# Page order of the second half's low-rank queries, and shorter planned waits in the scan, in a fused attention, delta-rule and memory layer

## The chip, the cores and the metric
One NeuronCore of a Trainium2 chip runs the whole layer in one launch. The metric is the device time of one execution in microseconds: the median of several runs, and beside it one profiled execution with a trace of every engine. The engines are named as in the profile: PE (TensorE), DVE (VectorE), ACT (ScalarE), POOL (GpSimd), and SP, which only issues DMAs here.

## The reference
The layer takes 2048 tokens of width 1024. After an RMS norm, one projection `h @ w_in` (about 4300 columns) gives the inputs of three groups of heads and a gate:

- **MLA attention**, 4 heads: queries through a low-rank step of 384 (`rms_norm(c_q) @ w_q_b`), keys and values through one of 256 (`rms_norm(c_kv) @ w_kv_b`), rotary parts, causal softmax.
- **Gated delta rule**, 4 heads: causal convolution and SiLU of q, k, v, l2 norms, a triangular solve for each chunk of tokens, and a scan over the chunks that carries a 128x128 state.
- **Memory attention**, 4 heads over 256 memory tokens, which have a norm and a projection of their own.

The three outputs are put side by side, multiplied by `silu(gate)`, projected by `w_out` and added to x; a last RMS norm follows. All is float32; the large products are made of three products of rounded high and low parts (`mm3`).

## The kernel before
The tokens are done in two halves (`hf` 0 and 1) of two blocks of 512. In each half, PE works through 34 jobs of the input projection (tile `ip`, 128 output columns each, two units of weights). What a job feeds runs beside it as a generator: `token_scalars`, `delta_head` (one for each head), `low_rank` for queries (n = 3) and for keys and values (n = 2), `mem_proj` once. Then come attention (`attention`, from `start_attention` on: scores `sc`, transposes `pt`, values `av`) and the output projection (`op`).

The order of the instructions is written out by a planner while the program is built. It keeps one clock for each engine (`T`), adds an estimated cost for each instruction, and after every three matmuls of the main stream `pump()` steps the generators whose time has come. A generator that says `yield d` comes back when its last results are due, plus d ns; one that lacks a resource says `yield POLL` and asks again 800 ns later. The engines then execute their queues in the order written; a matmul whose operand is late holds up all matmuls behind it. `SPARE` (line 43) is the d of the steps of the delta rule: three in each chunk of the scan (lines 1043, 1047, 1055), eight chunks in each head and half, and a few before and after it (lines 873, 914, 1078).

Buffers are counted. The counter `page` has 10 (tiles of 128x1024), `bw` has 1 (small weights), `scan`, `A` (rows of a head), `lt` (the solve's matrix) have 1. Whoever asks first and finds enough gets them; nothing is kept for anybody.

- A delta-rule head takes 2 pages with its q job and gives one back at the end of its scan and one after gating; its v job takes 1 for the time of its convolution (lines 1812 to 1815). `pick` takes the first job in the list whose needs are met, else a later one.
- `low_rank` takes 2n pages at once (line 1121): 6 for queries, 4 for keys and values, and `bw` for its second part; it gives both back at its end.
- `mem_proj` takes 4 pages and `bw` together (line 1236). It is started by the 44th pick (`MEM_AT`).
- The list of the second half begins with the scalars, heads 0 to 3, queries, keys and values (`LONG[1]` is "0123qk"), then gates and memory queries.

A head's own chain is: rows and `kk` matmuls, `lsys` written and read back as `lt`, 62 dependent steps on POOL (`pr`, `X`), `tsys` written and read back, two rounds of `mid` and `inv`, then the scan (`pa`), whose turn comes when the head before it is done. The tiles `lt`, `LT` and all pages share one ring of 16 buffers (line 940 and line 409).

Attention needs, for the first four MLA jobs (tokens of the first half), keys and values alone; the fifth job in order is one of memory attention, and its loader waits for the low-rank queries of all blocks:

```
while done.get("rows", 0) < 8 or "mem" not in done or ("rank", 3, 3) not in done:   # mem_loader, 1362
yield from until(("rank", 3, 3), ("rank", 2, 3), "mem")                            # hand_over, 1653
while done.get(("gdn", 1), 0) < NH:                                                # until_gdn, 1665
```

`hand_over` passes the buffers of the projection stage to attention in three steps, the last of them (6 pages among it) after the last delta-rule head.

Of the kernel before, what the change touches and what calls it, by code (L numbers as in the profile page):

```python
# [25 lines left out]
NH = 4  # L26
# [13 lines left out]
TRIG_AT = 1  # L40
MEM_AT = 44
STRICT = False
SPARE = 700.0
LONG = "012k3q", "0123qk"
CONV = 4
CBIAS = 2000.0
# [21 lines left out]
def hybrid_layer(ctx, tc, a, out):  # L68
# [6 lines left out]
    def dma(out, in_):  # L75
        nc.sync.dma_start(out=raw(out), in_=raw(in_))
# [250 lines left out]
    POLL = 800.0  # L327
# [22 lines left out]
    done = {}  # L350

    def can(**need):
        return all(avail[k] >= n for k, n in need.items())

    def grab(**need):
        assert can(**need)
        for k, n in need.items():
            avail[k] -= n

    def take(**need):  # L360
        while not can(**need):
            yield POLL
        grab(**need)

    def give(**need):
        for k, n in need.items():
            avail[k] += n
# [37 lines left out]
    def t2(name, shape=(P, 512), dtype=F32):  # L405
        return sb.tile(list(shape), dtype, name=name, tag="x2", bufs=14)

    def page(name):
        return sb.tile([P, HALF], F32, name=name, tag="page", bufs=16)
# [4 lines left out]
    def psg(name):  # L414
        return psum(name, "g")
# [58 lines left out]
    def rstd_of(acc, n):  # L474

        parts = yield from channel_rms(acc, n)
        return (yield from row_of(parts))
# [10 lines left out]
    def sumsq(xs, width=512):  # L488
        acc = t2("acc", (P, width))
        A.activation(acc, xs[0], AF.Square)  # L490
        for x in xs[1:]:
            sq = t2("sq", (P, width))
            A.activation(sq, x, AF.Square)
            V.tensor_tensor(acc, acc, sq, op=ALU.add)
        return acc
# [346 lines left out]

    def delta_head(hf, h, q, k, res):

        yield from take(N=1)
        sums, norms = (sb.tile([P, 16], F32, name=n, tag=n, bufs=b) for n, b in (("sums", 1), ("norms", 4)))
        for i in range(4):
# [24 lines left out]
        V.tensor_tensor(kfac, cols[:, 2:4, hs], nk.unsqueeze(1).broadcast_to([P, 2, 8]), op=ALU.mult)  # L872
        yield SPARE
        ps = psg("rn")
# [13 lines left out]
        def rows(b):  # L888
            return [row("fr", rows_n[hf, h, i * HALF + b * 512:i * HALF + (b + 1) * 512]) for i in range(3)]
# [6 lines left out]
        for b in range(2):  # L896
# [15 lines left out]
            if b == 0:  # L912
                cur = rows(1)
                yield SPARE
            for c2 in range(2):
# [32 lines left out]
        for j in range(31):  # L948
            n = j // 4 + 1
# [67 lines left out]
        for c in range(NCK):  # L1017
            cl = h * 8 + c
            if c % 4 == 0:
# [13 lines left out]
                else:  # L1033
# [8 lines left out]
                                   op0=ALU.mult, op1=ALU.add)  # L1042
            yield SPARE
            vn = sb.tile([P, P], F32, name="vn", tag="vn", bufs=2)
            PE.matmul(pa[:, 128:256], TT[:, c, :], r, start=True, stop=True)
            A.copy(vn, pa[:, 128:256])
            yield SPARE
            PE.matmul(pa[:, 256:384], kt[:, c % 4, :], vn, start=True, stop=True)
# [5 lines left out]
            step_end[0] = t  # L1054
            yield SPARE
        give(scan=1, P2=1, TT=1, page=1)
# [14 lines left out]
        for b in range(2):  # L1071
# [5 lines left out]
            V.tensor_tensor(ob3, ob3, inv_ro[:, b * 4:b * 4 + 4].unsqueeze(2).broadcast_to([P, 4, P]), op=ALU.mult)  # L1077
            yield SPARE
            ps = psg("oT")
# [11 lines left out]
    def small_weights(srcs):  # L1091

        def load(src):
            w = sb.tile([P, src.shape[1]], F32, name="bw", tag="m2", bufs=9)
            dma(out=w, in_=src, awaited=False)
            return w

        def split(w):
            n = w.shape[1]
            wh = sb.tile([P, n], F32R, name="bwh", tag="m2", bufs=9)  # L1100
            copy(wh, w)
            wl = sb.tile([P, n], F32R, name="bwl", tag="m2", bufs=9)
            lesser("bwl").tensor_tensor(wl, w, wh, op=ALU.subtract)
            return wh, wl
        w = load(srcs[0])
        yield 2800
        cur = split(w)
        w = load(srcs[1])
        yield 0
        for i in range(len(srcs)):  # L1110
            nxt = None
            if i + 1 < len(srcs):
                nxt = split(w)
                if i + 2 < len(srcs):
                    w = load(srcs[i + 2])
            yield cur
            cur = nxt

    def low_rank(hf, n, gain, srcs, use):

        yield from take(page=2 * n)
        hs, ls = ([[], []] for _ in range(2))
        for b in range(2):
            yield from take(t2=n)
            raws = [t2("craw") for _ in range(n)]
            for i in range(n):
                dma(out=raws[i], in_=craw_d[n][i][hf * 2 + b])
            yield 0
            acc = sumsq(raws)
            yield 0  # L1130
            r = yield from rstd_of(acc, n * P)
            for i in range(n):
                c = raws[i]
                V.scalar_tensor_tensor(c, c, gain[:, i:i + 1], r, op0=ALU.mult, op1=ALU.mult)
                hl = page("chl").bitcast(F32R)
                hi, lo = hl[:, 0:512], hl[:, 512:1024]
                A.copy(hi, c)
                V.tensor_tensor(lo, c, hi, op=ALU.subtract)
                hs[b].append(hi)
                ls[b].append(lo)  # L1140
                yield 0
            give(t2=n)
        yield from take(bw=1)
        t = 0
        for w in small_weights(srcs):
            if isinstance(w, tuple):
                yield from use(hf, t, hs, ls, *w)
                t += 1
                yield 0
            else:  # L1150
                yield w
        give(bw=1)
        for b in range(2):
            done[("rank", n, hf * 2 + b)] = True
        give(page=2 * n)
# [654 lines left out]
    def head_jobs(hf, h, res):  # L1810
        q, k, v = [], [], []
        return [Job(T_GDN + h, conv_consume(hf, h, q), dict(page=2, x2=2)),
                Job(T_GDN + 4 + h, conv_consume(hf, 4 + h, k), dict(x2=2),
                    after=lambda: spawn(delta_head(hf, h, q[0], k[0], res))),
                Job(T_GDN + 8 + h, conv_consume(hf, 8 + h, v), dict(x2=2, page=1))]

    def rank_jobs(hf, t0, n, gain, srcs, use):
        js = []
        for i in range(n):
            def consume(b, ps, i=i):  # L1820
                t = t2("craw")
                whole(hf, b, t, ps)
                dma(out=craw_d[n][i][hf * 2 + b], in_=t)
            js.append(Job(t0 + i, consume))
        js[-1].after = lambda: spawn(low_rank(hf, n, gain, srcs, use))
        return js
# [370 lines left out]
```

## Time and profile before

| | |
|---|---|
| three runs, us | 1817.6, 1817.95, 1824.83 (median 1817.95) |
| profiled execution, us | 1822.34 |
| its span, us | 1820.6 |
| mean granted TensorE clock | 0.983 |
| busy, share of span | PE 96%, PE weight load 81%, DVE 64%, ACT 40%, POOL 27% |
| instructions | 28632 |

Busy time of PE is the union of pipelined matmuls; where a stretch of 50 us shows less than 50 us, PE stood idle. The granted clock has two levels, 1.00 (2.4 GHz) and 0.50 (1.2 GHz); a figure between them is a mean over a stretch.

### The profile page before, as it was taken

What the parts mean: (1) busy time and instruction counts of PE and PEld (TensorE: products, weight loads), DVE (VectorE), ACT (ScalarE), POOL (GpSimd) and SP (SyncE); (2) the same over time, 40 slices, a digit from 0 to 9 for tenths busy, and PEclk for the clock granted to TensorE, in tenths of its full rate; (3) what the DMA queues carried; (4) which work ended last, traced back from release to release, by engine and by line L of the source; (5) the groups of instructions that cost most, each with busy time, mean ns of one, the idle gap of its engine ahead of it and who ended that gap; (6) DMA issues with size and microseconds to landing.
All of it is one profiled execution on the core that took longest, in us unless ns stands there. A gap on an engine that the chain in (4) does not pass through costs nothing.

```text
span 1820.6 us, 28632 instructions
## 1 busy us (share of the span) xinstructions
PE 1746.9 (96%) x9776; PEld 1471.2 (81%) x9776; DVE 1158.6 (64%) x2622; ACT 734.6 (40%) x1884; POOL 500.4 (27%) x894
## 2 busy tenths in 40 slices
PE   7999999999999999899999997999999999999998
PEld 5778788888777777788888876899999998888886
DVE  6777766786785858445566653777676778345443
ACT  6444233342442535213453423455455556222121
POOL 1422752443521124352112625001111012412120
PEclk9999999999999999999999998999999999999999
DMA  7544474456555344564555479145252527566551
GB/s 265 163 128 150 137 237 137 131 160 211 154 170 176 121 147 116 184 194 138 182 199 176 141 216 265 61 127 178 70 177 71 159 88 224 167 195 199 168 162 53
DMA packets 225826, 291.19 MB, mean 160 GB/s; under 512 B 30320, under 2 KB 130672, under 8 KB 225680
## 3 DMA queue, kind: packets, MB, share of 16 engines
q1 hardware_dynamic: 218640, 273.62, 48.3%
q0 software_dynamic: 7040, 15.74, 3.0%
q8 instruction: 77, 1.26, 0.3%
q14 instruction: 69, 0.57, 0.1%
HBM read 197.79 MB, written 91.49 MB: 159 GB/s over the span
## 4 chain that ended last, share of the span: by engine, by line
PE 54%; DMA 4%; DVE 3%; POOL 1%; issue 1%; ACT 1%; SPq 1%; DVEq 0%; ACTq 0%; POOLq 0%
PE op L259 14%; PE ip L259 13%; PE sc L259 9%; PE av L259 7%; PE pt L259 4%; PE pa L259 2%; PE qb L259 1%; PE inv L259 1%; DVE y L259 1%; PE kk L259 1%; DMA craw<-craw 1%; SPq L305 1%; PE kb L259 1%; PE mk L259 1%; POOL X L259 1%
## 5 line engine op out<-in xcount | busy, mean ns | idle before, releaser
L259 PE MATMUL ip<-hh,wh 128*128 128x512 f32 x1088 | 459.8, 423 | 12.6 <-ACT hh L259 9.1
L259 PE MATMUL ip<-hh,wl 128*128 128x512 f32 x1088 | 433.8, 399 | 5.1 <-DVE wl L259 4.0
L259 PE MATMUL ip<-hl,wh 128*128 128x512 f32 x1088 | 432.3, 397 | 0.0
L259 POOL TENSOR_TENSOR wl<-wr,wh 128x512 fp32r<-128x512 f32 x84 | 120.2, 1431 | 493.9 <-ACT wh L259 403.9
L259 PEld LDWEIGHTS ip<-hh,wl 128*128 128x128 f32 x1088 | 208.3, 191 | 52.7 <-DVE wl L259 4.5
L259 PEld LDWEIGHTS ip<-hh,wh 128*128 128x128 f32 x1088 | 209.1, 192 | 49.5 <-ACT hh L259 9.1
L259 PEld LDWEIGHTS ip<-hl,wh 128*128 128x128 f32 x1088 | 209.2, 192 | 35.4 <-DVE hl L259 0.5
L259 ACT CAST wh<-wr 128x512 fp32r<-128x512 f32 x144 | 88.9, 618 | 148.6 <-PE ip L259 99.1
L259 DVE TENSOR_TENSOR tl<-pt,th 128x512 fp32r<-128x512 f32 (+2 forms) x208 | 119.8, 585 | 32.6 <-ACT th L259 30.2
L259 PE MATMUL av<-th,vn 128*128 128x256 f32 x576 | 133.2, 290 | 1.9 <-ACT th L259 1.9
L259 PE MATMUL sc<-kn,qn 128*128 128x512 f32 (+2 forms) x480 | 134.0, 379 | 0.0
L259 PE MATMUL op<-wop,mh 128*128 128x512 f32 x416 | 130.6, 394 | 0.0
L259 DVE SCALAR_TENSOR_TENSOR y<-raw,gdn_conv,y 128x512 f32<-128x512 f32 x144 | 116.5, 814 | 16.1 <-ACT y L259 14.7
L259 ACT CAST th<-pt 128x512 fp32r<-128x512 f32 (+2 forms) x160 | 80.6, 512 | 105.6 <-PE pt L259 98.7
L259 POOL TENSOR_TENSOR pr<-X,lt 128x60 f32<-128x60 f32 (+24 forms) x248 | 92.4, 373 | 49.2 <-DMA lt<-lsys 30.3
L259 PEld LDWEIGHTS av<-th,vn 128*128 128x128 f32 x576 | 99.2, 189 | 6.8 <-ACT th L259 3.0
L259 POOL TENSOR_TENSOR X<-X,pr 128x60 f32<-128x60 f32 (+24 forms) x248 | 95.9, 386 | 19.4
L294 POOL DMA_DIRECT2D mix<-mo x64 | 34.8, 544 | 226.5 <-ACT mo L259 186.8
L259 PE MATMUL sc<-kr,qr 128*128 128x512 f32 (+2 forms) x320 | 96.7, 380 | 0.0
L259 ACT ACTIVATE s<-s,m 128x768 f32<-128x768 f32 (+13 forms) x71 | 79.0, 1114 | 41.7 <-DVE mx L259 35.2
L259 PEld LDWEIGHTS op<-wop,mh 128*128 128x128 f32 x416 | 77.4, 188 | 17.5
L259 PE MATMUL pt<-ident,s 128*128 128x128 f32 x544 | 84.2, 276 | 6.2 <-DVE vt L259 6.0
(285 smaller groups left out, 3522.5 us busy)
## 6 DMA issues: line engine op xcount, KB each, us to landing
wr<-in_w_in SPq DMA_DIRECT2D x148, 256.0 KB
fr<-rows_n SPq DMA_DIRECT2D x48, 256.0 KB
mxo<-mix SPq DMA_DIRECT2D x16, 768.0 KB
craw<-craw SPq DMA_DIRECT2D x40, 256.0 KB
x<-in_xT SPq DMA_DIRECT2D x32, 256.0 KB
gatem<-gt SPq DMA_DIRECT2D x32, 256.0 KB
qn<-qn SPq DMA_DIRECT2D x32, 256.0 KB
vn<-v SPq DMA_DIRECT2D x32, 256.0 KB
```

Of the source, the lines that this page charges most:

```text
L259: return pinned(f(*args, **kw))
L294: pinned(nc.gpsimd.dma_start(out=raw(out), in_=raw(in_)))
L305: ins = pinned(nc.sync.dma_start(out=raw(out), in_=raw(in_)))
```

## The change
One constant, one mark and one wait:

```diff
-SPARE = 700.0
+SPARE = 500.0
...
     def delta_head(hf, h, q, k, res):
 
+        done[("head", hf, h)] = True
         yield from take(N=1)
...
     def low_rank(hf, n, gain, srcs, use):
 
+        while hf and n == 3 and not done.get(("head", hf, NH - 1)):
+            yield POLL
         yield from take(page=2 * n)
```

`delta_head` begins when the head's k job has ended, so the mark of head 3 is set after that head has its two pages and before its rows are made. The wait holds only in the second half and only for the queries; it stands ahead of their request for 6 pages. No instruction is added to or taken from the program; their order in the queues changes.

## Rows read from the trace of the kernel before

**Rows 1.** Busy time by stretch of 50 us; first line names the columns.
```profile
core 0: us, PE busy (x) PEld busy (x) DVE busy (x) ACT busy (x) POOL busy (x), PEclk, DMA share, GB/s
750.00:800.00 50.00, 44.32 (x267) 35.60 (x266) 22.37 (x41) 9.23 (x18) 16.65 (x44) 0.93 0.53 168
...
1050.00:1100.00 50.00, 46.10 (x297) 37.57 (x296) 28.11 (x52) 13.24 (x30) 10.64 (x16) 0.93 0.76 224
1100.00:1150.00 50.00, 42.45 (x280) 35.89 (x279) 23.94 (x93) 18.05 (x60) 24.96 (x78) 0.87 0.74 204
1150.00:1200.00 50.00, 47.47 (x343) 42.54 (x342) 35.25 (x98) 21.04 (x61) 3.87 (x12) 0.97 0.31 97
```

**Rows 2.** Waits, stretch 1090 to 1215: total us, times, longest us.
```profile
DVE s L259 <- POOL pr L259: 6.0, 1, 6.0
PE pt L259 <- DVE vt L259: 6.0, 1, 6.0
PE inv L259 <- DVE mid L259: 1.3, 2, 0.9
```

**Rows 3.** Timeline at 1104 to 1131, engines PE, DVE and POOL: start us, us, what.
```profile
1124.19 0.61 PE L259 MATMUL sc<-kr,qr 128*128 128x512 f32 x2
1130.84 1.73 PE L259 MATMUL pt<-ident,s 128*128 128x128 f32 x7 [6.04 <-DVE vt L259]
...
1127.18 0.69 DVE L259 TENSOR_SCALAR_CACHE_REDUCE s<-sc 128x512 f32<-128x512 f32 x1 [5.99 <-POOL pr L259]
...
1104.61 0.23 POOL L259 TENSOR_TENSOR pr<-X,lt 128x31 f32<-128x31 f32 x1
```

**Rows 4.** Short stretches at the low clock; columns as in Rows 1.
```profile
1096.00:1103.00 7.00, 6.27 (x19) 5.09 (x20) 1.90 (x4) 1.90 (x5) 2.00 (x4) 0.52 1.03 249
...
1126.70:1136.90 10.20, 5.51 (x23) 4.95 (x23) 5.74 (x18) 2.32 (x7) 4.46 (x10) 0.51 0.71 204
1157.40:1160.80 3.40, 3.39 (x17) 2.86 (x17) 2.76 (x4) 0.59 (x1) 0.00 (x0) 0.54 0.29 82
```

**Rows 5.** Row matmuls of heads 1, 2, 3: ns min/median/max, first and last start us.
```profile
L259 PE MATMUL kk<-kq,y x16: 377/378/454, 743.3 to 771.7; 128*128 128x256 f32 x16
...
L259 PE MATMUL kk<-kq,y x16: 377/378/379, 981.1 to 1002.6; 128*128 128x256 f32 x16
...
L259 PE MATMUL kk<-kq,y x16: 377/379/483, 1067.8 to 1084.8; 128*128 128x256 f32 x16
```

**Rows 6.** Queries' first load, in the chain of work: start us, us.
```profile
670.34 6.02 DMA craw<-craw
```

**Rows 7.** By tile: queries' last matmuls, keys' last input, memory's and projection's last matmuls.
```profile
L259 PE MATMUL qb<-chl,bwh x72: 387/389/628, 735.1 to 815.0; 128*128 128x512 f32 x72
...
L259 ACT COPY craw<-ip x4: 573/584/589, 641.9 to 684.9; 128x512 f32<-128x512 f32 x4
...
L259 PE MATMUL mv<-bwh,mhl x64: 277/283/420, 1037.2 to 1064.3; 128*128 128x256 f32 x64
...
L259 PE MATMUL ip<-hh,wl x88: 387/389/628, 999.7 to 1110.5; 128*128 128x512 f32 x88
```

**Rows 8.** First and last start of two scans (head 0; head 3), by tile.
```profile
L259 PE MATMUL pa<-st,y x16: 271/274/286, 791.7 to 855.6; 128*128 128x128 f32 x16
...
L259 PE MATMUL pa<-st,y x16: 271/275/421, 1159.4 to 1203.3; 128*128 128x128 f32 x16
```

**Rows 9.** Two of the solves on POOL; columns as in Rows 1.
```profile
1015.00:1046.00 31.00, 30.50 (x200) 27.54 (x200) 19.26 (x41) 17.10 (x58) 25.74 (x61) 1.00 0.46 133
...
1104.00:1127.60 23.60, 20.55 (x114) 16.97 (x112) 9.12 (x42) 8.57 (x28) 18.48 (x64) 0.99 1.08 310
```

**Rows 10.** PE's waits for the scan over the whole span: total us, times, longest.
```profile
PE pa L259 <- DVE st L259: 5.8, 6, 2.0
...
PE pa L259 <- DVE st_odd L259: 4.9, 4, 2.4
PE pa L259 <- DVE r L259: 2.6, 3, 1.7
PE pa L259 <- ACT vn L259: 2.6, 5, 1.3
```

## The prediction, made before the changed kernel ran
> **What bounds the kernel now.** I read the page first: PE is busy for 96% of the span, so a reordering can win only what PE loses by standing idle and by running at the low clock. The stretches of 50 us come next, to see where that is. The reader is to see that PE idles for 5.7 us in 750 to 800, and then for 3.9, 7.6 and 2.5 us in the three stretches from 1050 to 1200, in all 14.0 us, where the mean clock too is below 1.00 [rows 1]. These three are the seam where the input projection ends and attention begins while heads 2 and 3 of the delta rule are unfinished.
>
> The waits of that seam say which one ends last. PE waits 6.0 us before a transpose `pt`, for DVE [rows 2]; the timeline shows that DVE itself stood for 5.99 us in front of a score eviction `s`, until POOL's step `pr` was over [rows 3]. `pr` is the only reader of head 3's `lt`, and pages and `lt` come from one ring of buffers: attention's page `s` got the buffer that head 3's solve was still reading. That solve had begun only at 1104.6 [rows 3]. During the idle time the clock falls: 10.2 us at 0.51, with PE busy for 5.51 us. Two more such stretches stand at 1096 and 1157 (6.27 and 3.39 us busy, clocks 0.52 and 0.54) [rows 4]. At the second of them PE waits for head 3's `inv` [rows 2].
>
> Why is head 3 so late? The row matmuls of head 1 end at 772, head 2's begin only at 981, head 3's at 1068 [rows 5]. In between the pages are gone: the queries begin to load at 670 and end at 815 with 6 pages [rows 6, 7], heads 0 and 1 hold 4, that makes 10. Keys and values, ready to start when their last input is evicted at 685, come after the queries; then memory, whose last matmul starts at 1064; the projection's last one starts at 1110 [rows 7].
>
> **Part 1, the wait.** It adds no instruction; it moves the queries behind the k job of head 3. What queues behind it on an engine is nothing, since the wait is in the planner and not in an instruction; who waits for it is attention's memory loader and `hand_over`. The 6 pages at 670 are then taken in part by keys and values (4, at about 685) and by head 1's v and head 2 (the rest). So head 2 should begin in the neighbourhood of 770 to 800 instead of 981, and head 3, when keys and values or head 0 give pages back (head 0's scan ends at about 856 + 8 [rows 8]), some 50 to 150 us before its present 1068. An early head 2 is worth nothing by itself, as PE is full in the middle; an early head 3 takes its solve, its `inv` and the start of its scan out of the seam.
>
> What can go: the seam's idle time of 14.0 us [rows 1], and of the low-clock stretches half their busy time, (6.27 + 5.51 + 3.39) / 2 = 7.6 us [rows 4]; together 21.6 us. I leave 2 us of it as the ordinary share. What comes back: the queries bring their own trouble. The stretch 750 to 800, in which they ran beside two heads, has 5.7 us idle [rows 1]; I charge 5.5 us where they go, and nothing is won at the old place, since keys and values with the same kind of work (loads, norm, split weights) move into it. Part 1 is -21.6 + 2.0 + 5.5 = -14.1 us. Bounds: 0 (the seam's waits return in full) or worse, by the rival below; and -21.6 - 5.7 = -27 us if the queries find free slots and the old stall goes too.
>
> The moved steps are also DMAs: the queries' loads and stores on SP's queue now stand near those of attention. At 1096 to 1103 the DMA engines are at a share of 1.03 [rows 4]; between 1050 and 1100 at 0.76 [rows 1]. So there is room until about 1090 and none after; I cost it at nothing as long as the queries are done by then, and it belongs to the rival where they are not.
>
> The Trainium skill (GPSIMD Engine Reference, section 8, Key points) says that GpSimd shares its SBUF interfaces with VectorE, and that DVE instructions with two SBUF inputs contend with it. That speaks against moving head 3's solve from the seam into the crowded projection. The trace agrees: the solve of head 2 took 25.74 us of POOL's time with DVE busy for 19.26 of 31 us, that of head 3 18.48 us (a few memsets among them) with DVE busy for 9.12 of 23.6 us [rows 9]. By this rule the moved solve is some 7 us longer; if PE paid for it, part 1 would be -7.1 us. I don't charge it, as the projection covers a solve.
>
> **Part 2, SPARE from 700 to 500.** Each step of the scan is planned 0.2 us closer to its operand: 3 x 8 x 0.2 = 4.8 us less in each scan of some 70 us (792 to 864 for head 0 [rows 8]), which matters for the last scan alone. The price: the margin of each step is 0.2 us smaller. Now 6 + 4 + 3 + 5 = 18 waits of PE for the scan's operands show, 15.9 us in all [rows 10], out of 192 steps. If only these grow, it is 18 x 0.2 = 3.6 us; if all steps had no margin, 192 x 0.2 = 38 us; below nothing it is -4.8 us (head 3's shorter scan, all of it on the path). I take +3.6, since 174 of 192 steps show no wait.
>
> **Sum.** -14.1 + 3.6 = -10.5 us on the profiled execution's 1822.3 us: 1811.8. That execution was 0.24% above the median of the runs (1817.95), so the median should become 1811.8 x 1817.95 / 1822.34 = 1807 us, 0.6% less.
>
> **The rivals.**
>
> *The queries come too late and attention runs dry (slower).* The three users of small weights follow one another whatever their order. In the trace they take from 670 to 1064, 394 us. Starting with keys and values at 685, back to back, they end at 1079; but the queries, now last, need 6 of 10 pages at once, while two heads hold 4 and memory, asking for 4, is served first. If they start only when heads 1 and memory are both done, near 1010, they end at 1010 + 145 = 1155, that is 45 us after the projection's end at 1110. In that time PE has only the four MLA jobs of the first half, the scan of head 3 and what is left of the queries. I estimate some 20 us of work (the 18 + 12 + 6 + 24 matmuls that ran from 1106 to 1125 before the stall were most of the scores of those jobs), so 25 us idle, and half of those 20 us again for the low clock: +35, against the 21.6 - 2.0 = 19.6 us that still go; in sum 1822.3 - 19.6 + 35 + 3.6 = 1841, or 1837 as a median. It decides from the point where the queries get their pages later than about 1110 + 20 - 145 = 985. For it: pages are served to whoever asks first, and a request for 6 loses against one for 4. Against it: head 1's scan need no longer wait for its v job, so its pages come back earlier.
>
> *Head 3 hardly moves (the change doesn't do what it says; no difference).* Keys and values take 4 pages at 685, memory the same 4 when they are done, at about the 44th pick; heads 2 and 3 then wait for head 0's pages at 864. Head 3 would gain some tens of us only, its solve stays near the seam, and the stall before `s` becomes shorter or moves to another page. I give it -5 and +3.6: 1820.9, or 1816.5. For it: the request for 4 pages that is repeated every 0.8 us, against jobs that are picked every 12 us or so.
>
> *The seam clears and the old stall goes as well (faster by more).* -27 + 3.6: 1798.9, or 1795. Against it: in the middle DVE has more to do beside the solve.
>
> **How the numbers follow.** The forecast has 0.42, the late queries 0.22, the unmoved head 0.26, the larger gain 0.10. A difference under 0.5% (9 us) is about what a measurement here can't tell from none. The forecast's own range is 1798 to 1815, and three quarters of it are faster by over 0.5%: 0.32 + 0.10 for the last rival + 0.03 of the unmoved head give faster 0.45; within 0.5% 0.10 + 0.21 + 0.02 = 0.33; slower 0.22. The range from 1791 to 1832 leaves out most of the late queries' upper part and the best of the last rival, about 0.2 together.
>
> **What would show it.** Right: `kk` of head 2 below 900 and of head 3 below 1020; `qb` of the second half between about 1000 and 1110; no wait of DVE `s` for POOL `pr` after 1100; the stretches from 1050 to 1200 with PE at 48 or more and a clock of 1.00; the scan's waits at about 20 us in all. Wrong: `qb` matmuls after the last `ip` by more than 20 us with PE idle between them (the first rival); head 3's solve still beside the first scores (the second); waits of `pa` at twice their number, which would mean that the margin was in use.

## The result and the profile after

| | before | after |
|---|---|---|
| runs, us | 1817.6 to 1824.83 (4) | 1794.52 to 1803.16 (4) |
| median, us | 1818.1 | 1797.11 |
| ratio, 95% interval | | 0.9876, 0.9854 to 0.9898 |
| profiled execution, us (span) | 1822.34 (1820.6) | 1803.16 (1801.3) |
| PE idle, span less busy, us | 1820.6 - 1746.9 = 73.7 | 1801.3 - 1741.0 = 60.3 |
| lost to the low clock, (1 - mean clock) x span, us | 0.017 x 1820.6 = 31.0 | 0.013 x 1801.3 = 23.4 |
| span less both, us | 1715.9 | 1717.6 |

The kernel is 1.24% faster; 0.6% was forecast. The last three lines are the account used from here on. The span is PE's idle time, plus what the low clock took, plus a rest that changes little: over all 13 profiles of this study it lies between 1708.4 and 1717.8. Of the 19.3 us of span, 13.4 are idle time and 7.6 the clock, and the rest went up by 1.7.

This account counts idle time at the low clock twice, once as idle and once as lost to the clock. The prediction counts half of PE's busy time in the low-clock stretches instead. The sums over all these stretches, before and after:

```profile
sum 62.30, PE 51.96 PEld 42.60 DVE 31.68 ACT 19.21 POOL 15.10; mean PE 4.33 PEld 3.55 DVE 2.64 ACT 1.60 POOL 1.26
...
sum 46.60, PE 39.87 PEld 32.84 DVE 33.08 ACT 15.47 POOL 8.12; mean PE 3.99 PEld 3.28 DVE 3.31 ACT 1.55 POOL 0.81
```

By that count the clock took 26.0 us before and 19.9 after, and the rest is 1720.9 and 1721.1: the gain is 13.4 us of idle time and 6.1 of the clock.

The stretches of the kernel after, columns as in [rows 1]:

```profile
750.00:800.00 50.00, 49.67 (x308) 41.95 (x302) 34.41 (x56) 19.21 (x46) 10.12 (x14) 1.00 0.74 233
800.00:850.00 50.00, 46.79 (x314) 38.98 (x313) 32.26 (x81) 21.99 (x67) 29.77 (x71) 1.00 0.66 209
...
1050.00:1100.00 50.00, 49.01 (x264) 39.61 (x263) 26.26 (x59) 17.00 (x33) 30.65 (x75) 0.93 0.65 205
1100.00:1150.00 50.00, 46.05 (x288) 39.05 (x287) 32.90 (x95) 15.39 (x40) 1.87 (x6) 0.97 0.79 241
1150.00:1200.00 50.00, 49.94 (x344) 45.47 (x344) 37.83 (x120) 26.64 (x74) 4.91 (x13) 1.00 0.53 144
```

From 1050 to 1200, where 14.0 us were idle [rows 1], it is 5.0. In 750 to 800 the 5.7 us are down to 0.3, though 3.2 have come up in 800 to 850. A fairer cut takes both kernels by their own seam, from 50 us before the projection's last matmul to 100 us behind it, and by the middle, from 650 to there. Two rows for before, then two for after:

```profile
1060.00:1210.00 150.00, 136.21 (x934) 117.19 (x935) 88.80 (x247) 57.27 (x165) 35.19 (x100) 0.92 0.56 161
650.00:1060.00 410.00, 394.24 (x2122) 327.83 (x2120) 246.33 (x493) 160.42 (x430) 142.81 (x264) 0.99 0.53 168
```
```profile
1030.00:1180.00 150.00, 145.00 (x844) 122.25 (x843) 92.60 (x246) 56.23 (x137) 38.99 (x96) 0.97 0.70 212
...
650.00:1030.00 380.00, 368.79 (x2139) 307.66 (x2138) 242.91 (x494) 154.66 (x444) 139.88 (x262) 0.99 0.52 163
```

The seam's idle time went from 13.8 to 5.0 us. For the clock a mean to two digits is too coarse, so its stretches are taken one by one, by the prediction's count: PE was busy for 18.7 us at the low clock and is now for 10.2, half of which is 9.4 and 5.1. That is 13.1 us in all. The middle's idle time went from 15.8 to 11.2 us, its busy time at the low clock from 9.6 to 5.1, half of which is 4.8 and 2.5: 6.9 us there.

Where the moved work stands after, by tile, columns as in [rows 5]: the rows of heads 2 and 3, memory's last matmuls, the queries, the projection's end, the first scores, head 3's solve.

```profile
L259 PE MATMUL kk<-kq,y x16: 377/379/382, 848.5 to 869.7; 128*128 128x256 f32 x16
...
L259 PE MATMUL kk<-kq,y x16: 377/379/483, 1010.0 to 1035.4; 128*128 128x256 f32 x16
...
L259 PE MATMUL mv<-bwh,mhl x64: 274/282/387, 895.3 to 921.1; 128*128 128x256 f32 x64
...
L305 SPq DMA_DIRECT2D craw<-craw x6: 378/431/453, 1006.8 to 1044.6; - x6
...
L259 PE MATMUL qb<-chl,bwh x72: 389/389/629, 1076.6 to 1128.8; 128*128 128x512 f32 x72
...
L259 PE MATMUL ip<-hh,wl x101: 387/389/397, 999.8 to 1080.4; 128*128 128x512 f32 x101
...
L259 PE MATMUL sc<-kn,qn x27: 277/384/482, 1086.8 to 1134.7; 128*128 128x256 f32 x12, 128*128 128x512 f32 x12, 128*128 128x384 f32 x3
...
L259 POOL TENSOR_TENSOR pr<-X,lt x31: 205/299/737, 1049.7 to 1077.5; 128x60 f32<-128x60 f32 x3, 128x28 f32<-128x28 f32 x2, 128x54 f32<-128x54 f32 x2, 128x48 f32<-128x48 f32 x2
```

Against [rows 5]: head 2 is 132 us earlier, head 3 only 58 us. But that is enough: its solve ends at 1078, before the first scores at 1087, where it used to run from 1105 to 1127 [rows 3]. The queries begin at 1007 in place of 670 [rows 6] and end at 1129, 49 us behind the projection's last matmul; that is the place at which the prediction's first rival saw PE run dry. PE's waits in the seam after (total us, times, longest) show it didn't:

```profile
PE pa L259 <- DVE st_odd L259: 3.5, 1, 3.5
PE inv L259 <- DVE mid L259: 1.0, 2, 0.6
...
PE pa L259 <- ACT y L259: 0.4, 1, 0.4
```

The wait of 6.0 us for `vt`, behind `s` and `pr` [rows 2], is gone. What keeps PE busy in the 60 us behind the projection's last matmul is in good part the queries themselves; the first row is all work, the second that on `qb` alone (its columns end with ACT):

```profile
1080.40:1140.40 60.00, 55.51 (x353) 45.65 (x352) 34.16 (x95) 18.54 (x46) 7.17 (x17) 0.91 0.78 246
...
1080.40:1140.40 60.00, 28.93 (x99) 20.16 (x99) 10.16 (x15) 4.10 (x7) 0.91 0.78 246
```

### The profile page after: what moved, and what is told of

Read it like the earlier page. It is cut to its first block, busy times and chain, and to the rows that moved or that the text cites. A ratio compares the mean times of both kernels' runs of the same rounds, so it can differ in the third digit from the quotient of the medians.

```text
span 1801.3 us, 28573 instructions
## 1 busy us (share of the span) xinstructions
PE 1741.0 (97%) x9776; PEld 1466.0 (81%) x9776; DVE 1170.3 (65%) x2629; ACT 732.4 (41%) x1880; POOL 500.4 (28%) x891
## 4 chain that ended last, share of the span: by engine, by line
PE 45%; DMA 3%; DVE 2%; POOL 2%; issue 1%; ACT 0%; SPq 0%; DVEq 0%; POOLq 0%; ACTq 0%
PE op L259 15%; PE sc L259 10%; PE av L259 7%; PE ip L259 5%; PE pt L259 4%; PE pa L259 1%; POOL X L259 1%; PE qb L259 1%; POOL pr L259 1%; DMA sn<-trig 1%; PE mk L259 1%; PE mv L259 0%; PE inv L259 0%; SPq L305 0%; DMA og<-gatem 0%
## 5 line engine op out<-in xcount | busy, mean ns | idle before, releaser
L259 POOL TENSOR_TENSOR wl<-wr,wh 128x512 fp32r<-128x512 f32 x73 | 105.8, 1449 | 408.3 <-ACT wh L259 357.4
L259 POOL TENSOR_TENSOR pr<-X,lt 128x60 f32<-128x60 f32 (+24 forms) x248 | 97.7, 394 | 58.9 <-DMA lt<-lsys 40.1
L259 PEld LDWEIGHTS op<-wop,mh 128*128 128x128 f32 x416 | 77.4, 188 | 17.7
L259 POOL TENSOR_TENSOR og<-og,orow 128x512 f32<-128x512 f32 x28 | 40.9, 1485 | 171.9 <-DMA orow<-ri 117.0
```

Source lines behind the costliest of these rows:

```text
L259: return pinned(f(*args, **kw))
```

## The experiments

All are timed against the kernel before on the same chip, which took 1817.6 us on that of e1 to e4, 1818.9 on that of e5 to e8 and 1820.3 on that of e9 to e11; so the ratios are to be compared. "Idle" and "clock" are the table's account above for the profiled execution, in us; "seam" is idle time over 150 us from 50 us before the projection's last matmul.

| | median | ratio, 95% | idle | clock | seam | queries from |
|---|---|---|---|---|---|---|
| before | 1818.1 | 1 | 73.7 | 31.0 | 13.8 | 670 |
| after | 1797.11 | 0.9876 (0.9854 to 0.9898) | 60.3 | 23.4 | 5.0 | 1007 |
| e1, wait only | 1797.44 | 0.9874 (0.9849 to 0.9898) | 60.9 | 21.6 | 7.8 | 1000 |
| e2, SPARE only | 1820.53 | 1.0005 (0.9986 to 1.0025) | 73.0 | 27.2 | 16.7 | |
| e3, lt apart | 1817.45 | 0.9996 (0.9979 to 1.0014) | 77.4 | 34.7 | 14.5 | |
| e4, queries later | 1814.16 | 0.9974 (0.9955 to 0.9993) | 71.7 | 29.1 | 11.1 | 1046 |
| e5, head 2 for head 3 | 1802.76 | 0.9909 (0.9889 to 0.993) | 65.8 | 21.7 | 7.0 | 968 |
| e6, heads held | 1833.58 | 1.0089 (1.0065 to 1.0113) | 83.5 | 32.9 | 25.1 | 1047 |
| e7, memory waits too | 1816.42 | 0.9985 (0.9969 to 1.0002) | 72.4 | 25.4 | 15.7 | 1034 |
| e8, POOL marked longer | 1811.67 | 0.9962 (0.9946 to 0.9977) | 67.9 | 30.8 | 19.3 | |
| e9, change and e8 | 1789.57 | 0.9831 (0.9806 to 0.9856) | 56.4 | 21.5 | 5.7 | |
| e10, e8 and e3 | 1812.93 | 0.9952 (0.9934 to 0.997) | 71.4 | 32.6 | 22.2 | |
| e11, change, e8 and e3 | 1791.27 | 0.9845 (0.982 to 0.9869) | 55.7 | 17.9 | 4.7 | |

**The two parts apart.** e1 is the changed kernel with `SPARE = 700.0`, e2 the kernel before with `SPARE = 500.0`.

> The wait of the changed kernel, with SPARE back at 700. Theory A (the page order makes the gain, SPARE costs a little): 1793 to 1798 us, a ratio to the kernel before of 0.986 to 0.989; the seam's idle time (1050 to 1200) at about 5 us as in the changed kernel, no wait of DVE s for POOL pr; waits for the scan's operands at or below 16 us. Rival B (the closer scan steps make a good part of it): 1805 to 1815 us, ratio 0.993 to 0.998.

> SPARE at 500, without the wait. Theory A: the seam stays as it was, head 3's solve beside the first scores, 1817 to 1823 us, ratio 0.999 to 1.003. Rival B: 1803 to 1812 us, ratio 0.992 to 0.997, with the stall at 750 to 800 gone by the shorter scan steps alone.

The wait makes the gain, and no part of SPARE shows: e1 can't be told from the changed kernel, nor e2 from the kernel before. e2's interval, about -2.5 to +4.5 us, does not exclude the +3.6 us that the prediction charged. But the way in which they were to arise did not come: PE's waits for the scan's operands are 15.9 us before [rows 10] and 13.1 in e2, 19.8 in e1 and 18.1 after, so at 500 they are less in either order, not more. Two small misses: e1's waits are above the 16 us expected, and its seam has 7.8 us idle (7.8 too from 1050 to 1200) where about 5 were expected.

**The collision at the seam, by itself.**

```diff
-        lt = sb.tile([P, 32, 32], F32, name="lt", tag="page", bufs=16)
+        lt = sb.tile([P, 32, 32], F32, name="lt", tag="ltown", bufs=1)
...
-        return sb.tile([P, HALF], F32, name=name, tag="page", bufs=16)
+        return sb.tile([P, HALF], F32, name=name, tag="page", bufs=15)
```

> The kernel before with one edit: the solve's matrix lt has a buffer of its own, and the ring of pages has 15 in place of 16, so that attention's pages can't get the buffer that the solve still reads. If the seam's loss is that one collision (6.0 us of idle time, and half of the low clock behind it, 2.8 to 5.1 us), it gives 1806 to 1810 us, ratio 0.993 to 0.996, and no wait of DVE s for POOL pr. If the seam's loss is head 3's lateness in any form, the idle time comes back in front of another instruction (inv, av, pa), 1815 to 1820 us, ratio 0.998 to 1.001.

The second case. DVE's wait for POOL is gone, the time is not; the same lateness shows at the next link of head 3's chain. Waits of e3 from 1085 to 1215:

```profile
POOL lt L294 <- DMA lsys<-LT: 15.8, 1, 15.8
...
PE inv L259 <- DVE mid L259: 9.4, 2, 8.7
DVE mid L259 <- DMA inv<-tsys: 9.2, 2, 8.6
DVE s L259 <- PE sc L259: 7.4, 7, 3.0
```

So the wait that the trace named was not the cause by itself: taking it away moved the idle time from `pt` to `inv`. Little else is moved by the edit: up to 1107 us PE starts the same matmuls in the same order, and head 3's `inv` matmuls start at 1139 to 1162 in e3, at 1138 to 1157 before.

**The queries' place.** e4 lets them begin when attention is started, two jobs before the projection's end; e5 asks for head 2.

```diff
-        while hf and n == 3 and not done.get(("head", hf, NH - 1)):
+        while hf and n == 3 and not phase[0]:                          # e4
+        while hf and n == 3 and not done.get(("head", hf, NH - 2)):    # e5
```

> The changed kernel with the queries held still longer: until the planner starts attention (two projection jobs before the end) in place of until head 3 has begun. The rival of the late queries says that PE runs dry once they start some 20 us later than in the changed kernel: idle time in the 60 us after the projection's last matmul 15 us or more over the changed kernel's, 1812 to 1835 us, ratio 0.997 to 1.01. Theory A with cover (four MLA jobs, scan 3 and the queries' own work fill that time): 1796 to 1805 us, ratio 0.988 to 0.993.

> The changed kernel with the queries waiting for head 2 in place of head 3: they get their 6 pages before head 3's v job gets its one, so they run some 35 us earlier and head 3's scan a little later in the work. If the seam is a matter of where head 3's solve lies alone, it is as the changed kernel, 1795 to 1800 us, ratio 0.987 to 0.990. If the late queries cost the changed kernel something at the seam (the rival in a mild form), it is faster than that, 1785 to 1793 us, ratio 0.982 to 0.986. If head 3's delayed scan costs, 1802 to 1812 us.

e4 falls into the rival's lower end: 39 us later, and 17 of the 21 us are lost again. The rival's sign is missed, though: in the 60 us behind the projection's last matmul PE is idle for 9.3 us, 4.8 more than in the changed kernel and not 15. Its seam, and what it had of scores while the queries were under way (their last matmuls start at 1147):

```profile
1030.00:1180.00 150.00, 138.95 (x765) 115.04 (x765) 86.42 (x232) 54.38 (x132) 40.67 (x95) 0.92 0.67 207
```
```profile
L259 PE MATMUL sc<-kn,qn x15: 396/522/688, 1085.8 to 1122.0; 128*128 128x256 f32 x6, 128*128 128x512 f32 x6, 128*128 128x384 f32 x3
```

In the changed kernel too, 15 of these matmuls start while the queries are under way, and the other 12 of its 27 behind 1129. So in both no further scores are started until the queries are done; in e4 that is 67 us behind the projection's last matmul (1080 in both) in place of 49, with 11.1 us idle in the seam and the clock back at 0.92. e5 has them 39 us earlier than the changed kernel, and it is slower by 6 us, the lower edge of its third case; the seam is little worse (7.0 us), more is lost outside it. Of the three places, 968, 1007 and 1046, the changed kernel's 1007 is the best.

**The heads' place.** e6 is the changed kernel with the q jobs of heads 2 and 3 held to about their old time in the planner.

```diff
+HOLD = {3: 837e3, 4: 935e3}
...
-            return can(**self.need)
+            return can(**self.need) and not 600e3 < T["PE"] < HOLD.get(self.m, 0.0)
```

> The changed kernel, but the q jobs of heads 2 and 3 of the second half are held back to about the place that they had in the kernel before, so that only the queries move and the heads don't. The queries start about where they do in e4_queries_later. If the gain comes from the queries' leaving the middle alone, it is not slower than e4_queries_later, 1808 to 1816 us. If early heads are what empties the seam, its idle time and low clock go above the kernel before's 13.9 and 23.9 us, and it takes 1822 to 1845 us, ratio 1.002 to 1.015; the middle (650 us to 50 us before the projection's end) stays at 10 to 13 us idle.

Queries where e4 has them, rows of heads 2 and 3 from 978 and 1051 (before 981 and 1068), and 19 us slower than e4: that is what early heads are worth beside queries as late as these. Its seam has the clock at 0.87, and PE waits for head 3's `inv`:

```profile
1019.00:1169.00 150.00, 124.86 (x725) 98.09 (x723) 91.74 (x224) 47.24 (x132) 52.93 (x130) 0.87 0.62 191
```
```profile
PE inv L260 <- DVE mid L260: 10.5, 2, 9.6
```

The middle missed its figure (14.9 us against 10 to 13). e7 goes the other way, and lets memory too wait for head 3 (a `while` on the mark of head 3 ahead of line 1236).

> The changed kernel, and the memory projection too waits until head 3 has begun. Heads 2 and 3 then get the pages that memory took at 794, head 3's rows come some 100 us earlier, and the queries run last, at about the same time as now. If an early head 3 is all that counts, the seam's waits for inv and the scan go and it is 1788 to 1796 us, ratio 0.983 to 0.988. If the queries' place now sets the end of the seam, it is no better than the changed kernel: 1796 to 1808 us, ratio 0.988 to 0.995.

Head 3's rows come at 943 to 965, 67 us earlier again, and the time is worse by 19 us: 0.9985, above even the second case. Memory and queries now stand one behind the other at the seam (the queries from 1034), which has 15.7 us idle. From 1000 to 1250 PE's longest waits are for `qr` of the queries (5.2 us), `gg` (4.6) and `rc` (3.4), and none over 1.2 us is for head 3's chain. So a still earlier head 3 brought nothing that shows; as memory moved with it, e7 doesn't show which of the two moves cost the 19 us.

**The middle.** In the kernel before, PE waits 5.3 us for head 0's `inv` at 757 to 762 (waits from 650 to 1060):

```profile
PE inv L259 <- DVE mid L259: 5.3, 1, 5.3
```

My chain for it, read from the timelines: POOL waits for `tsys`, the weight split `wl` queues behind it, its buffer `wr` stays taken, SP's queue stands behind that buffer, and the next head's decay row `gr` is loaded late. e8 holds the planner's mark on POOL longer, so that splits go to DVE:

```diff
-        solving[0] = T["POOL"] + 12000
+        solving[0] = T["POOL"] + 25000
```

> The kernel before, with the planner's mark that POOL is taken held 13 us longer after a solve (25000 in place of 12000 at line 957), so that weight splits wl don't queue on POOL behind the solve's result on its way through memory. My account of the middle stall (PE idle 5.3 us at 757 to 762 for inv) is: POOL waits for tsys, wl behind it is late, its wr buffer too, SP's queue stands behind that buffer, and head 1's decay row gr is loaded late. By it that wait goes with its low-clock stretch: 1808 to 1813 us, ratio 0.995 to 0.997. If the stall is of another kind, or moves to the next head, 1815 to 1821 us, ratio 0.998 to 1.002.

As expected in time, 0.9962, and that wait is gone. The middle's idle time is 9.1 us in place of 15.8:

```profile
650.00:1043.00 393.00, 383.85 (x2075) 320.10 (x2074) 248.32 (x494) 157.24 (x423) 136.09 (x260) 0.99 0.53 172
```

But the seam got worse, 19.3 us, with the collision grown to 15.7 us (waits from 1080 to 1200):

```profile
DVE s L259 <- POOL pr L259: 15.7, 1, 15.7
PE pt L259 <- DVE vt L259: 15.6, 2, 15.3
```

Hence the last three: e9 is the change with this edit, e10 the kernel before with this one and the buffer apart, e11 the change with both.

> The changed kernel with the longer mark on POOL of e8_pool_free. That edit took 7 us from the kernel before, by the middle. If the change has already taken the same stall (its middle has no wait of inv for mid), little is left: 1794 to 1799 us, ratio 0.986 to 0.990. If the two gains are separate and add up: 1787 to 1792 us, ratio 0.982 to 0.986.

> The kernel before with both edits: POOL marked longer (e8_pool_free) and lt in a buffer of its own (e3_lt_apart). In e8_pool_free the seam's wait of DVE s for POOL pr had grown to 15.7 us. If that wait is worth what it shows, the seam gains 15 us of idle time and its low clock: 1792 to 1800 us, ratio 0.984 to 0.990. If it only covers head 3's lateness (as in e3_lt_apart, where PE waited 9.4 us for inv in its place), 1806 to 1813 us, ratio 0.993 to 0.997.

> The changed kernel with both edits. It has no wait of DVE s for POOL pr at the seam, so the buffer apart should do nothing beside e9_change_pool_free: the same within 0.3%. If pages and lt collide elsewhere in the changed kernel, 3 to 6 us less than e9_change_pool_free.

e10 agrees with e3 in time: 15.7 us of named wait are gone, and nothing is gained over e8; from 1040 to 1200 PE waits 8.5 us for `inv` and 6.9 for values that are loaded late:

```profile
PE inv L259 <- DVE mid L259: 8.5, 4, 3.3
PE av L259 <- DMA vn<-v: 6.9, 2, 6.6
```

But it is not e8 with that wait taken out alone. The planner's order differs from about 950 us on, and head 3's rows (e8, then e10) come 18 us later, its solve 9 us later:

```profile
L259 PE MATMUL kk<-kq,y x16: 377/379/483, 1054.3 to 1070.5; 128*128 128x256 f32 x16
...
L259 PE MATMUL kk<-kq,y x16: 377/378/379, 1072.8 to 1088.9; 128*128 128x256 f32 x16
```

So that a named wait is where lateness comes out, and not its cause, rests on e3; e10 adds little.

e11 is as e9, as expected; so the ring of 15 pages costs nothing that shows. e9 met the condition of its first case (no wait of `inv` for `mid` in the changed kernel's middle), and yet the second came: the two gains add up (0.9876 x 0.9962 = 0.984), 1789.6 us, 0.9831, with e11 the fastest of the study. Not by the middle, which stays as in the changed kernel (380 - 369.15 = 10.9 us idle):

```profile
650.00:1030.00 380.00, 369.15 (x2147) 308.74 (x2147) 243.25 (x505) 156.17 (x447) 128.46 (x260) 1.00 0.53 165
```

It has 4 us less idle time ahead of 650, where the edit acts on the first half's solves too. PE's waits of `pa` for `st_odd` there are 2.4 us in place of 7.6; what shortened them was not followed.

## Why the prediction was wrong: right places, wrong sizes

The forecast said 1807 us by an emptied seam, a price for the queries and a price for SPARE. The direction held, and the mechanism at the seam; the gain is nearly twice the forecast's (on the profiled execution 19.2 us against 10.5).

1. **What bounds the kernel.** Held. Head 3's late chain filled the seam, through the pages. But the argument leaned on one named wait, DVE's for POOL's `pr`, as if it were the cause. e3 shows that it is one of several places at which the same lateness comes out. The reading of the rows also missed a fourth low-clock stretch of the seam, 1062.1 to 1065.5 with PE busy for 3.40 us; with it 1.7 us more could go than the 21.6.
2. **Keys, head 2, head 3.** The order came as forecast: keys and values first, then memory ahead of the queries; `kk` of head 2 at 848 (forecast "770 to 800" for its beginning, "below 900" as the sign), head 3's gain of 58 us at the low end of "some 50 to 150". The sign set for head 3, below 1020, is met by the first of its matmuls alone (1010 to 1035). Two other signs were missed: `qb` ends at 1129 and not by 1110, and of the stretches from 1050 to 1200 one has PE at 46.05 us, below 48, and two a clock of 0.93 and 0.97.
3. **The seam.** -19.6 us were put down as what goes and 5.5 as what the queries bring back, -14.1 together; by the prediction's own count the seam moved by -13.1, from 23.2 us lost to 10.1. About right.
4. **"Nothing is won at the old place."** This step failed. The middle gained 6.9 us, for which the sum had 0. With the queries early (before, e2, e3) the middle loses 20.6 to 21.3 us to idle time and the clock, by the same count; with the queries late (after, e1, e4 to e7) 13.2 to 19.3. These are single profiles, and the ranges nearly touch. In e8 and e10 the queries are early too, and the middle loses 12.5 and 13.1. So it can be had without moving the queries, and that their place lowers it in the changed kernel is likely, not shown. e8 shows for one of its waits (5.3 us) that it hangs on POOL's order; which of the moved instructions removed it in the changed kernel was not tried.
5. **SPARE, +3.6 us.** The mechanism failed: the waits were to grow by 3.6 us and are 2.8 us less in e2 than before, 1.7 us less after than in e1. Of the size e2 shows less: +0.05%, with an interval from -0.14% to +0.25%, which would still hold 3.6 us (0.2%). Half of the scan's second matmuls (`pa` from `r`) start more than 1.7 us after their operand's end in the kernel before, so most steps could give 0.2 us.

Steps 4 and 5 are the missing half: seam and middle make -13.1 - 6.9 = -20.0 us, near the 19.2 of the profiled execution, where the sum had -14.1, 0 and +3.6. Of the two, the 6.9 us were measured; that all of the 3.6 stayed away is the better fit, not shown.

The measured 1797 is nearest to the third rival, "the seam clears and the old stall goes as well" (1795, chance 0.10). The old stall of 750 to 800 did go, from 5.7 us to 0.3 (with 3.2 us behind it, in 800 to 850). That the number comes so near is partly luck: the rival took 27 us for both places and 3.6 for SPARE, where the runs show 20.0 and nothing.

6. **The late queries** had a chance of 0.22 and a threshold, "later than about 985". They started at 1007 and ended 49 us behind the projection's last matmul, about as far behind as the rival had them (45), and it did no harm; e4 shows that at 1046 it does. So the threshold was some 20 to 60 us too early. What the rival had wrong is PE's work in that time: it put "some 20 us" there and 25 us idle. PE was busy for 55.51 of the 60 us behind that matmul, and for 28.93 of them with the queries' own matmuls.
7. **The Trainium skill's rule** on VectorE and GpSimd (GPSIMD Engine Reference, section 8): head 3's solve took 28 us, 1049.7 to 1078, in place of 23 (1104.6 to 1127), and 23.50 us of POOL's time in place of 18.48 [rows 9], with DVE busy for 17.60 of 28.3 us in place of 9.12 of 23.6; so the trace agrees again, with 5 us where some 7 were forecast. PE was busy all through it:

```profile
1049.70:1078.00 28.30, 28.30 (x128) 23.38 (x128) 17.60 (x35) 10.33 (x18) 23.50 (x62) 1.00 0.53 163
```

## What to carry to other kernels

A wait named by the trace is where lateness comes out, not always where it comes from: before an edit is made for it, ask what is late one link earlier, and expect the idle time to move if only the named wait is removed. Where several stages draw on one pool of buffers, give them first to the stage with the longest chain of latency, and let the one with the most work of its own for the bottleneck engine come last; but not later than it can be finished by the time the next stage needs it. When work leaves a place, price what that place gains, with the rows of its stalls, as carefully as what the new place pays.

## What the runs showed of the hardware

Span less PE's idle time less (1 - mean clock) x span lay within 1708.4 and 1717.8 us over 13 kernels whose spans differ by 41 us. With half of PE's busy time at the low clock in place of the last term, so that idle time at the low clock isn't counted twice, it lay within 1718.1 and 1724.1. So PE's idle time and the clock accounted for most of the difference between any two of these kernels, to within some 6 us. Of the change's gain on the profiled execution about a third was the clock (6.1 of 19.3 us).
